# A two-layer mixer stack on one core: layer-0 scans with both directions in one tile, 64 x 64 matmuls, one mask per bank and the state's decay as a diagonal matmul

## The chip, the core and the metric

The kernel runs on one core of a Trainium2 chip, in one launch. The metric is the device time in microseconds. Three runs of the kernel before gave a median of 3486.47 us (3482.63 to 3488.52). The engines are named as in the profile: PE (matmuls), PEld (its weight loads), DVE (vector), ACT (scalar), POOL (GpSimd) and SP (which issues most transfers). PE's results go to PSUM, which the kernel divides into eight banks of 512 float32 columns.

## The reference, cut to what matters

A model with width 1024, 512 tokens (l) and 256 context tokens (c) runs through two layers of one kind and then two of another. The change is in the first layer's mixer, in its RWKV part: eight heads of 64 channels, each scanned over the context and then over the tokens, forwards and backwards.

```
def step(s, inp):                       # per head, s is [v, k]
    r_t, w_t, k_t, v_t, kk_t, b_t = inp
    sa = einsum('bhvk,bhk->bhv', s, kk_t)
    s = s * w_t - sa x b_t + v_t x k_t
    return s, einsum('bhvk,bhk->bhv', s, r_t)
for d in range(2):                      # direction 1 is reversed in time
    y_c, s_c = rwkv7_scan(*dir_inputs(prep_c, d), zeros)
    y_l, _   = rwkv7_scan(*dir_inputs(prep_l, d), s_c)
```

The same mixer has a spatial gate on the other half of the width, and both halves go through one output projection. The weights' GEMMs are split into two float32r parts, with three matmuls for a product.

## The kernel before, in words

**Chunks and blocks.** The scans work on chunks of 64 tokens. A strand of the program handles one pair of heads: head 0 lies on partitions 0 to 63, head 1 on 64 to 127. It goes through six blocks (two of the context, four of the tokens), and a block is two chunks (NB = 2) of each direction. So there are 4 x 6 = 24 blocks. A block has three parts.

`rwkv_prep` (L1009) loads keys, receptances and normalised keys (krk, one page per direction), makes two low-rank projections (`lora`, L1024; matmuls at L1030), the decays and their inverses, and the scaled operands b and kd (BK), direction by direction (L1069 to L1092). Then `products` (L1106) multiplies, per direction, chunk and head, 64 rows of [b, kd] (128 columns of weights) with 192 columns (decay matrix, r, kk): one matmul of the form 64 x 128 gives the token-major copies TM, the r products BI, and the kk products, from which the own half goes to W and the other half to KS. Each of these leaves PSUM through its own masked copy (L1116, twelve a block on DVE) or plain copy (L1122, four a block on ACT). L1137 multiplies kk with b again, in the other order, for L.

`Chunk.inverse` (L708) turns W into the transposed inverse of I + L by doubling, in five steps of two half steps. A half step is eight matmuls (four matrices, two heads) into one bank. Here the masked L and the intermediate product lie in padded pairs: head 0's page holds zeros on partitions 64 to 127 and the other way round, so that each matmul contracts 128 rows (form 128 x 64, L729 and L739). Masking on POOL (L721) and copying on ACT (L734) are one instruction per head. The second block kind of the kernel, from about 2300 us, calls the same function unpadded (form 64 x 64).

`rwkv_scan` (L1152) goes through two steps, in each one chunk of each direction: P = KS times [state over values], evicted by ACT to Pb; A = W times Pb, negated into NV by ACT and DVE; S = TM times NV, after which four DVE instructions (L1188, one per direction and head) decay the state with De and add S; and Y = BI times NV plus r times the old state, added to y.

**The order.** PE's order is fixed when the kernel is built. A strand is a generator: each `yield` states rough times (its own on PE, and the time until the next step finds its operands), and `tick` emits steps that are due between GEMM matmuls. Pairs 0 and 1 run under the projection and gate GEMMs; when these end (near 390 us), pairs 2 and 3 and a strand of modulation vectors (L539) start beside them. When pairs 0 and 1 have ended, `gemm_out` (L1269) starts its 288 GEMM matmuls beside the last blocks of pairs 2 and 3, and nothing of the mixer's output is normalised before pairs 2 and 3 have ended (`K.drain()`, near 920 us). Pairs 0 to 2 have two PSUM banks each; pair 3 has one, and a second when pair 0 ends.

Every product above is a float32 matmul, which the trace records as two passes. In the trace the passes of the two heads start within 0.01 us of each other and overlap.

## Time and profile before

| what | value |
|---|---|
| median of three runs | 3486.47 us |
| lowest, highest | 3482.63, 3488.52 us |
| profiled execution, its span | 3495.0 us |
| PE, DVE, ACT, POOL busy | 93%, 64%, 37%, 21% of the span |
| chain that ended last | PE 79%, DVE 12%, ACT 3%, DMA 2% |

The page gives no other time of the profiled execution than its span, which is 8.5 us above the median of the runs. The layer-0 scans lie in 120 to 925 us. A busy PE counts the time from a matmul's start to its modelled end, so that 90% is not 90% of its peak. The rows that matter are below.

### The profile page before, as it was taken

The page shows a single profiled execution, that of the slowest core. Times are in us where ns is not written, and L with a number is a line of the kernel's source. Part 1 is how long each engine was busy: PE and PEld are TensorE (multiplying, and loading weights), DVE is VectorE, ACT ScalarE, POOL GpSimd, SP SyncE. Part 2 cuts the span into 40 slices and gives each one's busy share as a digit, 9 for nine tenths or more (in the row PEclk, how much of TensorE's full clock was granted, in tenths as well). Part 3 has the DMA queues.
Part 4 walks back from the last instruction along what each step waited for, and adds up shares of the span by engine and source line. Part 5 has one row for each costly group of instructions (what it writes and reads, how often), then busy time and mean ns, then how long its engine had stood idle before and what let it go on. Part 6 is the DMA issues. An engine that isn't in the chain of part 4 may idle for free.

```text
span 3495.0 us, 60370 instructions
## 1 busy us (share of the span) xinstructions
PE 3253.1 (93%) x23708; PEld 2550.9 (73%) x23708; DVE 2231.2 (64%) x4937; ACT 1310.1 (37%) x2845; POOL 740.1 (21%) x982
## 2 busy tenths in 40 slices
PE   7999888979899999999988999988999998999998
PEld 5878666667678888877865788857767676766766
DVE  4544678774665555575666675767578566767655
ACT  4334344343342222246433332343333335234332
POOL 4222444432100000010000000004147100516600
PEclk8999989979899999999998999989999799999989
DMA  6432443531221212222222233232223153223333
GB/s 227 131 91 72 147 148 125 170 106 48 79 71 61 64 57 68 91 75 69 82 64 91 85 100 118 91 92 76 76 85 101 59 184 91 75 65 98 97 107 113
DMA packets 300511, 335.99 MB, mean 96 GB/s; under 512 B 25774, under 2 KB 246076, under 8 KB 300228
## 3 DMA queue, kind: packets, MB, share of 16 engines
q1 hardware_dynamic: 298116, 329.69, 29.6%
q8 instruction: 187, 3.06, 0.4%
q0 software_dynamic: 2112, 2.45, 0.3%
q14 instruction: 96, 0.79, 0.1%
HBM read 282.13 MB, written 49.94 MB: 95 GB/s over the span
## 4 chain that ended last, share of the span: by engine, by line
PE 79%; DVE 12%; ACT 3%; DMA 2%; issue 2%; POOL 1%; SPq 0%; DVEq 0%; POOLq 0%; ACTq 0%
PE mm L329 20%; PE mm L332 18%; PE mm L333 18%; PE ps L729 3%; PE ps L739 2%; PE ps L1164 2%; DVE cfa L1756 2%; PE ps L1110 2%; PE ps L539 1%; PE ps L371 1%; PE ps L2107 1%; DVE wl L78 1%; PE ps L1681 1%; PE ps L406 1%; PE ps L2094 1%
## 5 line engine op out<-in xcount | busy, mean ns | idle before, releaser
L329 PE MATMUL mm<-hl,wh 128*128 128x512 f32 (+1 forms) x3296 | 1254.4, 384 | 40.6 <-DVE qkv L1756 15.0
L332 PE MATMUL mm<-hl,wh 128*128 128x512 f32 (+1 forms) x3296 | 1224.6, 372 | 1.7 <-DVE hl L468 1.6
L333 PE MATMUL mm<-hl,wl 128*128 128x512 f32 (+1 forms) x3296 | 1216.6, 371 | 0.0
L329 PEld LDWEIGHTS mm<-hl,wh 128*128 128x128 f32 x3296 | 631.3, 192 | 181.8 <-issue 38.0
L333 PEld LDWEIGHTS mm<-hl,wl 128*128 128x128 f32 x3296 | 631.5, 192 | 113.5 <-issue 2.3
L332 PEld LDWEIGHTS mm<-hl,wh 128*128 128x128 f32 x3296 | 633.1, 192 | 101.5 <-DVE hl L468 3.2
L77 ACT ACTIVATE wh<-wr 128x512 fp32r<-128x512 f32 (+3 forms) x718 | 367.3, 561 | 680.8 <-PE mm L332 599.2
L78 DVE TENSOR_TENSOR wl<-wr,wh 128x512 fp32r<-128x512 f32 (+3 forms) x718 | 433.3, 637 | 220.8 <-ACT wh L77 199.7
L1334 DVE SCALAR_TENSOR_TENSOR cv<-mm,vecs,cv 128x441 f32<-128x441 f32 (+2 forms) x352 | 243.2, 692 | 94.1 <-ACT cv L1322 87.8
L1385 POOL MEMSET gwh<- 128x1024 f32 x3 | 2.9, 956 | 963.6 <-PE mm L332 963.6
L721 POOL TENSOR_TENSOR cut<-bk,zm 64x256 f32<-64x256 f32 x180 | 135.6, 753 | 145.4 <-PE ps L729 78.5
L1756 DVE SCALAR_TENSOR_TENSOR cfa<-ld,vecs,cfa 128x497 f32<-128x497 f32 (+14 forms) x160 | 151.2, 945 | 18.6 <-ACT cfa L1750 16.4
L1923 POOL TENSOR_SCALAR tap<-ld,vecs 128x498 f32<-128x498 f32 (+4 forms) x80 | 147.5, 1843 | 51.6 <-DVE kq L1982 12.4
L1357 DVE TENSOR_TENSOR fy<-fy,mm 128x512 f32<-128x512 f32 x96 | 55.2, 576 | 126.5 <-PE mm L333 125.7
L734 ACT ACTIVATE pad<-ps 64x256 f32<-64x256 f32 (+1 forms) x160 | 69.1, 432 | 152.0 <-PE ps L729 149.5
L1924 POOL TENSOR_TENSOR cfa<-cfa,tap 128x498 f32<-128x498 f32 (+4 forms) x80 | 115.8, 1447 | 5.5
L2099 ACT ACTIVATE u<-ps,beT 64x128 f32<-64x128 f32 x128 | 46.3, 362 | 153.1 <-DVE u L2098 152.0
L1110 PE MATMUL ps<-krk,bk 64*128 64x192 f32 x384 | 85.9, 410 | 13.9 <-ACT cut L1122 6.0
L351 POOL TENSOR_TENSOR rs<-var,mhalf 128x4 f32<-128x4 f32 (+1 forms) x26 | 28.8, 1107 | 313.9 <-DVE var L349 313.7
L729 PE MATMUL ps<-cut,cut 128*64 128x64 f32 x1440 | 92.4, 237 | 1.8 <-POOL cut L721 0.8
L1336 ACT ACTIVATE cv<-cv,vecs 128x256 f32<-128x256 f32 (+1 forms) x66 | 43.0, 652 | 133.2 <-DVE cv L1334 78.4
L729 PEld LDWEIGHTS ps<-cut,cut 128*64 128x64 f32 x1440 | 75.0, 147 | 13.6 <-issue 8.2
(479 smaller groups left out, 4761.3 us busy)
## 6 DMA issues: line engine op xcount, KB each, us to landing
ar<-in_ada_w_dram SPq DMA_DIRECT2D x96, 512.0 KB
wr<-in_ffn_up_dram SPq DMA_DIRECT2D x44, 1024.0 KB
wr<-in_w_in_dram SPq DMA_DIRECT2D x28, 1024.0 KB
ld<-sp SPq DMA_DIRECT2D x84, 256.0 KB
wr<-in_w_in_dram SPq DMA_DIRECT2D x32, 512.0 KB
xsp<-x SPq DMA_DIRECT2D x48, 256.0 KB
x<-xsp SPq DMA_DIRECT2D x48, 256.0 KB
wr<-in_ffn_down_dram SPq DMA_DIRECT2D x20, 512.0 KB
```

Source lines behind the costliest of these rows:

```text
L77: nc.scalar.activation(h[:, q:e], src, AF.Copy)
L78: nc.vector.tensor_tensor(l[:, q:e], src, h[:, q:e].bitcast(F32), SUB)
L329: mm = nc.tensor.matmul(ps[:m, :n], wh[:, i, :m], H[:, :n], start=first and i == 0, stop=False)
L332: nc.tensor.matmul(ps[:m, :n], wh[:, i, :m], L[:, :n], start=False, stop=False)
L333: nc.tensor.matmul(ps[:m, :n], wl[:, i, :m], H[:, :n], start=False, stop=last and i == nk - 1)
L721: nc.gpsimd.tensor_tensor(t[r].rearrange(T4, d=2, c=nb), Lp[r].rearrange(T4, d=2, c=nb), self.zm[s][r, ::-1].unsqueeze(2).to_broadcast([r. ...
L729: nc.tensor.matmul(ps[r, u * 64:u * 64 + 64], l[q, u], W[q, u], start=True, stop=True)
L1110: nc.tensor.matmul(ps[:, c], src, krk[d][hs[h]].rearrange("p x (c j) -> p x c j", c=NB)[:, :, c], start=True, stop=True)
L1334: nc.vector.scalar_tensor_tensor(t3[:, ro, co], a3[:, ri, ci], tap(ky, kx, ff), t3[:, ro, co], MUL, ADD)
L1756: nc.vector.scalar_tensor_tensor(dst[:, a:b], src[:, a + o:b + o], taps[j], dst[:, a:b], MUL, ADD)
L1923: nc.gpsimd.tensor_scalar(x[:, a:b], src[:, a + o:b + o], taps[j], None, MUL)
L1924: nc.gpsimd.tensor_tensor(g[:, a:b], g[:, a:b], x[:, a:b], ADD)
```

## The change

- b, kd, r, kk, decays and y of both directions lie in one tile each, so that what was done per direction is one instruction over 256 columns (`skew` gives access patterns that run over both directions' shifted decays; `both` and the y slice step from one direction's chunk to the other's). Two DVE instructions become ACT's (adding 1 to the decays' sigmoid, k_dir's scale and bias).
- `products` works with 64 x 64 matmuls: first, per head, b and kd times [r, kk] (128 columns) for all four chunks into one bank; one masked DVE instruction of 128 x 512 per bank (mask pm) then gives BI, the strict KS part and W's start. A second round (64 columns) with the diagonal decay matrices gives TM, after L1137's product. POOL's copies of kk into KS are two of 64 x 256 instead of four of 64 x 128. The low-rank matmuls are split into column halves.
- `inverse` is unpadded everywhere: 64 x 64 matmuls, one masking and one copy instruction for both heads.
- In the scan, the state's decay is a diagonal matmul into the bank of S (four more 64 x 64 matmuls a step), and two plain copies, one on ACT and one on DVE, take the new state out.
- The `yield` times of these steps are new. A strand of pairs 0 and 1 gets five half pages instead of six (the pool has 20, not 22), and the page with b and kd is freed before the scan, not after it. Comments and docstrings are removed, which shifts lines.

```diff
-        tri = K.const([P, 4, C64], name="tri")
...
+        pm = [K.const([P, 2, 2, C64], name="pm") for _ in range(2)]
+        nc.gpsimd.memset(pm[0], 1.0)
...
+            for d in range(2):
+                for x in range(2):
+                    sel(pm[0][r, d, x], [[1 - 2 * d, C64]], -x, 2 * d - 1)
+        nc.vector.tensor_copy(pm[1], pm[0])
...
+            nc.vector.tensor_copy(pm[h][r, :, 1], self.zm[1][r])
...
-            for r, _, t in own:
-                nc.gpsimd.tensor_tensor(t[r].rearrange(T4, d=2, c=nb), Lp[r].rearrange(T4, d=2, c=nb),
-                                        self.zm[s][r, ::-1].unsqueeze(2).to_broadcast([r.stop - r.start, 2, nb, C64]), MUL)
+            nc.gpsimd.tensor_tensor(Lm.rearrange(T4, d=2, c=nb), Lp.rearrange(T4, d=2, c=nb),
+                                    self.zm[s][:, ::-1].unsqueeze(2).to_broadcast([P, 2, nb, C64]), MUL)
...
-                for r, q, l in zip(hs, row, L):
-                    nc.tensor.matmul(ps[r, u * 64:u * 64 + 64], l[q, u], W[q, u], start=True, stop=True)
+                for r in hs:
+                    nc.tensor.matmul(ps[r, u * 64:u * 64 + 64], L[r, u], W[r, u], start=True, stop=True)
...
-            for r, z, _ in own:
-                nc.scalar.activation(z[r], ps[r], AF.Copy)
+            nc.scalar.activation(Zp, ps, AF.Copy)
...
+        for ds in (range(2),) if two else ((0,), (1,)):
+            ps = pss or {ds[0]: K.ps()[:, :n]}
+            for m in hs:
+                for d in ds:
+                    nc.tensor.matmul(ps[d][m], up[wkey][hs[d], m], at(lo[key], d)[hs[d]], start=True, stop=True)
+            for d in ds:
+                nc.scalar.activation(t[:, dsl(d)], ps[d], AF.Tanh, bias=K.v(bias, 4 * d + p), scale=0.5)
...
+    nc.vector.scalar_tensor_tensor(b, bI, 0.5, kk, MUL, MUL)
+    nc.vector.tensor_tensor(kI, kI, k, MUL)
+    nc.vector.tensor_tensor(kd, kI, iD, MUL)
...
+    for t, m in ((kk, skew(0, S + 1, C64)), (r, skew(1, S - 1, C64))):
+        t = t.rearrange(T4, d=2, c=NB)
+        nc.vector.tensor_tensor(t, t, m, MUL)
+    nc.vector.tensor_tensor(k.rearrange("p (u j) -> p u j", u=U), CH.i64.unsqueeze(1).to_broadcast([P, U, C64]),
+                            De.rearrange("p d c -> p (d c)").unsqueeze(2).to_broadcast([P, U, C64]), MUL)
...
-    def products(d, hh):
-        pss = [(h, K.ps()[:, :3 * n].rearrange("p (c x j) -> p c x j", c=NB, x=3)) for h in hh]
-        for c in range(NB):
-            for h, ps in pss:
-                src = BK[d][hs[h], c, h:h + 2].rearrange("p x j -> p (x j)")
-                nc.tensor.matmul(ps[:, c], src, krk[d][hs[h]].rearrange("p x (c j) -> p x c j", c=NB)[:, :, c],
...
-            masked(Wp[:, dsl(d)], own, 2, CH.zm[1][:, d])
-            masked(KS[h][d], opp, 2, CH.tri[:, 2 * d])
-            masked(BI[h][:, dsl(d)], slice(0, P), 1, CH.tri[:, 2 * d + 1])
-            nc.scalar.activation(TM[h][:, dsl(d)].rearrange(c4, c=NB), ps[:, :, 0], AF.Copy)
...
+    def products(hh, wd, rhs):
+        pss = {h: K.ps()[:, :U * wd] for h in hh}
+        for u in range(U):
+            for x in range(2):
+                for h in hh:
+                    src = (kd if x else b)[hs[h], 64 * u:64 * u + 64]
+                    nc.tensor.matmul(pss[h][hs[1 - h if x else h], wd * u:wd * u + wd], src, rhs(hs[h], u), start=True, stop=True)
+        return pss
...
+    for hh in ((0, 1),) if two else ((0,), (1,)):
+        pss = products(hh, 2 * C64, lambda q, u: KQ5[q, :, u])
+        for h in hh:
+            nc.vector.tensor_tensor(RK[h].rearrange("p (d c x) -> p d c x", d=2, c=NB),
+                                    pss[h].rearrange("p (d c x) -> p d c x", d=2, c=NB),
+                                    CH.pm[h].rearrange("p d x j -> p d (x j)").unsqueeze(2).to_broadcast([P, 2, NB, 2 * C64]),
+                                    MUL)
+        yield 500 * len(hh), 900
+    W = Wp[:, :2 * n].rearrange("p (u j) -> p u j", u=U)
+    KS = []
+    for h in range(2):
+        t = RK[h].rearrange(u4, u=U, x=2)[:, :, 1]
+        nc.vector.tensor_tensor(W[hs[h]], t[hs[h]], CH.i64[hs[h]].unsqueeze(1).to_broadcast([C64, U, C64]), ADD)
+        nc.gpsimd.tensor_copy(t[hs[h]], KQ5[hs[h], 1])
+        KS.append(t)
     ps = K.ps()
...
+    yield 320, 300
+    for hh in ((0, 1),) if two else ((0,), (1,)):
+        pss = products(hh, C64, lambda q, u: k[q, 64 * u:64 * u + 64])
+        for h in hh:
+            nc.scalar.activation(TM[h][:, :2 * n], pss[h], AF.Copy)
+        yield 320 * len(hh), 600
...
-        acc(pS, (lambda d, h: TM[h][:, u[d]], lambda d, h: NV[h][:, u[d]]))
-        for d in range(2):
-            for h in range(2):
-                q = hs[h]
-                nc.vector.scalar_tensor_tensor(SV[h][q, un[d]], SV[h][q, u[d]], De[q, d, cc[d]:cc[d] + 1], pS[q, d], MUL, ADD)
...
+        def decayed():
+            acc(pS, (lambda d, h: dg[hs[h], u[d]], lambda d, h: SV[h][hs[h], u[d]]), last=False)
+        if two:
+            decayed()
+        yield 320, 700
+        if not two:
+            decayed()
+        acc(pS, (lambda d, h: TM[h][:, u[d]], lambda d, h: NV[h][:, u[d]]), first=False)
+        nc.scalar.activation(slots(SV, 0, un), pS[hs[0]], AF.Copy)
+        nc.vector.tensor_copy(slots(SV, 1, un), pS[hs[1]])
...
+        t = y[s].rearrange("p (c j) -> p c j", j=C64)[:, o[0]:None if end < 0 else end:step]
+        if ("y", s, o[0]) in seen:
+            assert ("y", s, o[1]) in seen
...
```

PE's rows in the first scan step of the first pair (Pb: A's operand; the row after a row with the same tile is the same accumulation). Before (left out: the other strands' rows, and rows that repeat the pair above):

```order
L1164 MATMUL ps_2215<-Pb_2140,cut_1158 64x64 x4
...
L1164 MATMUL ps_2242<-cut_1156,cut_1160 64x64
L1164 MATMUL ps_2242<-cut_1157 64x64
...
L1164 MATMUL ps_2251<-cut_1159,cut_1156 64x64
L1164 MATMUL ps_2251<-cut_1160,cut_1157 64x64
...
L1164 MATMUL ps_2251<-krk_1296,cut_1155 64x64
L1164 MATMUL ps_2251<-krk_1296,cut_1156 64x64
```

The scan's own rows were A, S, then Y. Now, PE's rows at the same place (ps_2135 is S; its first four matmuls are the decay):

```order
L1176 MATMUL ps_2128<-Pb_2105,cut_1166 64x64 x4
L1176 MATMUL ps_2135<-cut_1161,cut_1163 64x64 x4
...
L1176 MATMUL ps_2135<-cut_1162,cut_1165 64x64
L729 MATMUL ps_2155<-pad_1641,bk_1684 64x64 x7
L1176 MATMUL ps_2135<-cut_1162,cut_1166 64x64
...
L1176 MATMUL ps_2165<-rk_1437,cut_1162 64x64
L1176 MATMUL ps_2165<-rk_1438,cut_1162 64x64
...
L1176 MATMUL ps_2165<-kq_1297,cut_1161 64x64 x4
```

The decay stands right behind A, in the same form (64 x 64), and S's product with TM (128 x 64) now meets a half step of the other strand's inverse in another form (L729, 64 x 64).

DVE's rows in the same step, before (cut_1157 is NV's second head, cut_1155 and cut_1156 the states, cut_1527 the other strand's W; the two L1188 rows come twice):

```order
L1181 TENSOR_SCALAR cut_1157<-ps_2215 64x2x64
L832 TENSOR_SCALAR kkv_2166<-ps_2161 128x8
L749 SCALAR_TENSOR_TENSOR k_2181<-mm_2029,vecs_109,k_2181 128x255
L1188 SCALAR_TENSOR_TENSOR cut_1155<-cut_1155,De_1321,ps_2242 64x64
L1188 SCALAR_TENSOR_TENSOR cut_1156<-cut_1156,De_1321,ps_2242 64x64
...
L740 TENSOR_TENSOR cut_1527<-cut_1527,ps_2265 128x256
```

The whole decay stood between NV and the other strand's row. DVE's rows of that step now (cut_1161 is the second head's state):

```order
L1195 TENSOR_SCALAR cut_1162<-ps_2128 64x2x64
L738 SCALAR_TENSOR_TENSOR k_2218<-mm_2082,vecs_109,k_2218 128x511
L730 TENSOR_TENSOR cut_1541<-cut_1541,ps_2155 128x256
L1208 COPY cut_1161<-ps_2135 64x128
L739 SCALAR_TENSOR_TENSOR k_2218<-mm_2082,vecs_109,k_2218 128x511
```

Four instructions have become one on DVE; the other half of the state is ACT's (L1207).

## Rows read from the trace of the kernel before

**Rows 1.** The page's part 4: shares of the chain that ended last, by engine

```profile
PE 79%; DVE 12%; ACT 3%; DMA 2%; issue 2%; POOL 1%; SPq 0%; DVEq 0%; POOLq 0%; ACTq 0%
```

**Rows 2.** Four stretches: length; busy PE, PEld, DVE, ACT, POOL; clock; DMA share; GB/s

```profile
180.00:390.00 210.00, 206.55 (x2075) 167.74 (x2076) 104.07 (x297) 80.16 (x196) 60.44 (x107) 1.00 0.30 90
390.00:680.00 290.00, 258.46 (x3774) 189.28 (x3773) 223.68 (x718) 118.99 (x390) 133.82 (x251) 0.88 0.44 145
680.00:780.00 100.00, 86.75 (x1347) 66.52 (x1343) 72.17 (x228) 42.73 (x132) 38.62 (x66) 0.86 0.43 129
780.00:925.00 145.00, 131.63 (x1376) 104.02 (x1377) 73.23 (x241) 47.57 (x133) 36.55 (x58) 0.90 0.15 47
```

**Rows 3.** Pieces of the chain of waits in 200 to 1000: start us, us, what

```profile
470.63 2.75 DMA krk<-rkv
...
776.75 2.65 DMA krk<-rkv
```

**Rows 4.** Timeline of PE from 694.46: start us, us, line, operation, shapes

```profile
694.46 0.44 PE L1137 MATMUL ps<-bk,krk 64*64 64x64 f32 x6
694.83 0.27 PE L729 MATMUL ps<-cut,pad 128*64 128x64 f32 x1
...
694.94 0.22 PE L729 MATMUL ps<-cut,pad 128*64 128x64 f32 x1
...
695.00 0.22 PE L729 MATMUL ps<-cut,pad 128*64 128x64 f32 x1
...
695.30 0.22 PE L729 MATMUL ps<-cut,cut 128*64 128x64 f32 x1
695.45 0.45 PE L1164 MATMUL ps<-Pb,cut 64*64 64x64 f32 x8
```

**Rows 5.** The same view: products of two heads at 833.79, of one at 432.07

```profile
432.07 0.92 PE L1110 MATMUL ps<-krk,bk 64*128 64x192 f32 x4
432.91 0.33 PE L739 MATMUL ps<-cut,bk 128*64 128x64 f32 x2
...
833.79 0.92 PE L1110 MATMUL ps<-krk,bk 64*128 64x192 f32 x8
834.64 0.50 PE L329 MATMUL mm<-hl,wh 128*128 128x512 f32 x1
```

**Rows 6.** The same view: 64 x 64 forms, both partition halves into one bank

```profile
260.73 0.68 PE L1137 MATMUL ps<-bk,krk 64*64 64x64 f32 x16
261.34 0.27 PE L1164 MATMUL ps<-cut,cut 128*64 128x64 f32 x1
...
2406.21 1.15 PE L729 MATMUL ps<-W,pad 64*64 64x64 f32 x32
```

**Rows 7.** DVE by line and shape, 160 to 960: xcount | busy us, mean ns | idle before

```profile
L1188 DVE SCALAR_TENSOR_TENSOR cut<-cut,De,ps 64x64 f32<-64x64 f32 x192 | 53.4, 278 | 21.6 <-PE ps L1164 18.9
L1116 DVE TENSOR_TENSOR cut<-ps,zm 64x128 f32<-64x128 f32 x92 | 26.3, 286 | 49.3 <-PE ps L1110 45.2 <-POOL cut L721 1.6 <-POOL bk L1103 1.0
L1089 DVE TENSOR_TENSOR krk<-krk,cut 128x128 f32<-128x128 f32 x92 | 25.3, 308 | 0.1
L1092 DVE TENSOR_TENSOR bk<-cut,cut 128x128 f32<-128x128 f32 x46 | 19.5, 424 | 0.0
L1073 DVE SCALAR_TENSOR_TENSOR cut<-cut,krk 128x128 f32<-128x128 f32 x46 | 14.3, 342 | 0.4 <-DMA krk<-rkv 0.3
L1133 DVE TENSOR_TENSOR cut<-cut,i 128x256 f32<-128x256 f32 x23 | 10.4, 451 | 0.0
...
L1246 DVE TENSOR_TENSOR gv<-ps,bs 128x512 f32<-128x512 f32 x4 | 2.7, 678 | 5.2 <-PE ps L1243 5.2
```

**Rows 8.** ACT by line and shape in the same stretch

```profile
L734 ACT ACTIVATE pad<-ps 64x256 f32<-64x256 f32 x120 | 45.3, 377 | 51.5 <-PE ps L729 49.1 <-PE ps L1164 0.5
L1180 ACT ACTIVATE cut<-ps 64x128 f32<-64x128 f32 x48 | 12.8, 268 | 24.8 <-PE ps L1164 24.3
L1141 ACT ACTIVATE bk<-ps 128x256 f32<-128x256 f32 x23 | 8.8, 383 | 15.9 <-PE ps L1137 15.1 <-PE ps L1110 0.7
```

More of the change, by code (lines that the diff above doesn't have):

```diff
@@ L737, in inverse @@
             for u in range(nu):
-                for r, q, z in zip(hs, row, Zv):
-                    nc.tensor.matmul(ps[r, u * 64:u * 64 + 64], X[q, u], z[q, u], start=True, stop=True)
+                for r in hs:
+                    nc.tensor.matmul(ps[r, u * 64:u * 64 + 64], X[r, u], Z[r, u], start=True, stop=True)
             nc.vector.tensor_tensor(Wp, Wp, ps, SUB)
@@ L875, in mixer_ab @@
         if p < 3:
-            strand(p - 1, p=6, h=6, halves=12)
+            strand(p - 1, p=6, h=5, halves=12)
         proj(p)
@@ new lines, in rwkv_prep, with both @@
+    loc_at = [o for _, o in loc]
+    def both(t, i):
+        o = [x // i for x in loc_at]
+        step = o[1] - o[0]
+        end = o[1] + (1 if step > 0 else -1)
+        return t.rearrange("p (c j) -> p c j", j=i)[:, o[0]:None if end < 0 else end:step]
+    bo = both(bon[s], n)
+    d2 = "p (d j) -> p d j"
+    if ("b", s, loc_at[0]) in seen:
+        assert ("b", s, loc_at[1]) in seen
+        rkp = K.p1(name="rk")
+        rk = rkp[:, :2 * n]
+        nc.vector.tensor_tensor(rk, r, kI, MUL)
+        nc.gpsimd.tensor_tensor(bo, bo, rk.rearrange(d2, d=2), ADD)
+        K.free(rkp)
+    else:
+        seen.update(("b", s, o) for o in loc_at)
+        nc.vector.tensor_tensor(bo, r.rearrange(d2, d=2), kI.rearrange(d2, d=2), MUL)
@@ new lines, in rwkv_prep @@
+    for t, m in ((kk, skew(0, S + 1, C64)), (r, skew(1, S - 1, C64))):
[3 more added lines that the diff above has]
+                            De.rearrange("p d c -> p (d c)").unsqueeze(2).to_broadcast([P, U, C64]), MUL)
+    K.free(csp, Dpp, bIp, kIp)
+    yield 250, 5000
+    RK = [K.p2(name="rk") for _ in range(2)]
+    TM = [K.p1(name="tm") for _ in range(2)]
@@ L1163, in acc @@
                 for h in range(2):
-                    nc.tensor.matmul(ps[hs[h], d], lhsT(d, h), rhs(d, h), start=i == 0 and d == 0,
-                                     stop=i == len(parts) - 1, skip_group_check=True)
+                    nc.tensor.matmul(ps[hs[h], d], lhsT(d, h), rhs(d, h), start=first and i == 0 and d == 0,
+                                     stop=last and i == len(parts) - 1, skip_group_check=True)
     for st in range(NB):
```

198 lines of the change are left out of this document (71 added, 127 removed).

## The prediction

> **What bounds the kernel now.** I read the chain that ended last first: PE holds 79% of it and DVE 12% [rows 1], so what counts is PE's time and the waits between PE's small groups of matmuls. The change touches only the layer-0 scans, so next I cut their time into stretches [rows 2]. In 180 to 390, where pairs 0 and 1 run under the projection GEMMs, PE is busy 206.55 of 210 us at full clock: only less PE work would help there. In 390 to 680 four strands and the modulation vectors run without GEMMs: PE is busy 258.46 of 290 us, DVE 223.68 of 290, and PE's granted clock is 0.88. In 680 to 780 two strands are left (PE 86.75 of 100, clock 0.86), and in 780 to 925 they share PE with `gemm_out` (131.63 of 145, clock 0.90). A clock of 0.88 means that the 1.2 GHz level had 24% of that stretch, the 2.4 GHz level the rest. So in the 535 us from 390 on PE stands idle for 31.5 + 13.3 + 13.4 = 58 us, and about 0.24 x 290 + 0.28 x 100 + 0.20 x 145 = 127 us pass at half clock. That is what a shorter chain can win, and PE is near enough to full that more work on it would cost.
>
> What sets the end of these 535 us is pairs 2 and 3: they start at 390, take six blocks one after the other, and `gemm_out`'s last matmuls and the norm wait for them. A block takes 535 / 6 = 89 us.
>
> **PE's own time.** Four edits change it.
>
> (1) Changes of form. PE's row-and-column form changes from 64 x 64 to 128 x 64 between 694.46 and 694.83 and back at 695.45 [rows 4]. Inside the 128 x 64 group a pair of passes starts every 0.06 us (694.94, 695.00). The first pass after the change is followed after 0.11 us (694.83 to 694.94), and the last is followed by the next form after 0.15 us (695.30 to 695.45). A change of form thus costs (0.11 - 0.06) + (0.15 - 0.06) = 0.14 us at full clock. I count the neighbours of different form in the two PE orders from the first product to the last matmul of `gemm_out`: 228 under the GEMMs, 407 between gate and `gemm_out` and 91 after, now 226, 293 and 85. That is 726 to 604, so 122 x 0.14 = 17 us less. The Trainium skill (TensorEngine Tiling (Array Packing), Key Properties) says that changing the tiling mode, not just the tile, drains the engine. It speaks against the change at one place, S with TM in 128 x 64 beside an inverse now in 64 x 64, and the trace agrees that a change is not free, at 0.14 us; but lora, products, inverse and A now share a form, and the count goes down.
>
> (2) The decay: 24 blocks x 2 steps x 4 matmuls x 2 passes = 384 passes, two side by side, so 192 x 0.06 = 11.5 us more. They stand behind A in A's form, so no change is added.
>
> (3) Products. A block has 8 matmuls of 192 columns in two passes. Two heads in turn, eight passes, take 834.64 - 833.79 = 0.85 us; one head alone takes 432.91 - 432.07 = 0.84 us for four passes [rows 5]. Side by side the second head is free. Without the change of form a pass takes (0.84 - 0.20) / 4 = 0.16 us. In the order 71 of the 192 matmuls stand beside the other head's, 37%, so a block is 0.37 x 1.28 + 0.63 x 2.56 = 2.1 us. Now there are 16 matmuls of 128 columns and 16 of 64. By 0.16 us for 192 and 0.06 for 64 columns, a pass of 128 is 0.11 us. No row shows two matmuls that share rows but write different column halves in the 64 x 64 form. If they run side by side, and the two heads too when they are in turn (222 of 384 and 137 of 384 in the order, 58% and 36%), a block is 0.58 x 0.88 + 0.42 x 1.76 + 0.36 x 0.48 + 0.64 x 0.96 = 2.0 us: no change. If they do not, everything doubles: 4.1 us, or 24 x 2.0 = 48 us more. The nearest rows are the padded passes of rows 4: two column halves, all rows in common, side by side. I take 0 and keep +48 as a bound. For the low-rank matmuls, twice as many with half the columns each, the same holds: 0, at worst 12 us more.
>
> (4) The unpadded doubling. Padded 128 x 64 pairs start every 0.06 us [rows 4]. In 64 x 64, 16 passes of L1137 take 261.34 - 260.73 = 0.61 us to the next form, so 7 steps of 0.06 and 0.2 around them; and the second block kind's unpadded half step of 32 passes takes 1.15 us with its tail [rows 6], again 0.06 a pair. So PE gains nothing from dropping the zeros. The Trainium skill (TensorEngine Tiling (Array Packing), Gotcha 1) says that different row tiles cannot access the same PSUM bank at the same time; unpadded, the two heads are two row tiles that write one bank. By that rule each of the 8 pairs would take 0.06 us more, in 240 half steps 115 us. The trace disagrees: rows 6 show just this form into one bank, at the pair's pace. It stays a rival with a small chance.
>
> PE in all: -17 + 11.5 + 0 + 0 = -6 us.
>
> **The chain between PE's groups.** Per block [rows 7, 8]:
> - State: four DVE instructions of 278 ns in a row, 1.11 us, become one on ACT (268 ns, the same shape as L1180) and one on DVE beside it: -0.84 us in each of two steps, -1.7.
> - Inverse: two ACT copies of 377 ns become one of 128 x 256 (L1141, 383 ns): -0.37 in each of five steps, -1.85. POOL's masks halve too; its work lies beside ACT's copy, the other product and DVE's subtraction, so I count nothing.
> - Masks: twelve L1116 of about 286 ns and W's 451 ns, 3.9 us, become two of 128 x 512 from PSUM (L1246, 678 ns) and two 64 x 256 priced as L1133: 2.3 us, -1.6.
> - Operands: four L1089, two L1092, two L1073, and two each of L1090 and L1070 priced as L1073: 1.23 + 0.85 + 3 x 0.68 = 4.1 us become six of 128 x 256, 2.7 us: -1.4.
>
> That is 6.5 us of 89 per block, and DVE loses about a third of its scan work. Pairs 2 and 3 pass six blocks: 39 us. I take 35, because the last block's steps lie under `gemm_out`, where PE is the limit. Under the projection GEMMs (180 to 390) I count nothing, since PE is full there; if it were not, 2 blocks x 6.5 would follow.
>
> Bounds: nothing at all if PE is the limit throughout, and 58 us idle plus half of 127 us at half clock, 121 us, if the chain no longer stops PE. The block's first loads of krk end the chain twice (2.75 and 2.65 us, [rows 3]) because their page was free only after Y; the page is now freed after the inverse. I count 0 and keep 6 x 2.7 = 16 us on the fast side. Waits that are added: TM's products need both banks back, so they wait for two masks in a row (1.4 us) and L's copy; queued behind them on PE are the other strands' steps. The copy of L, its mask on POOL and TM lie beside each other before the inverse, and I count 0; if TM's part, 0.36 x 0.48 + 0.64 x 0.96 = 0.8 us a block, were fully exposed on the late pairs, it would be 5 us.
>
> **Sum.** -6 - 35 = -41 us. The profiled execution spans 3495.0 us; that becomes 3454. It lies 8.5 us above the median of the runs, so the prediction is 3445 us.
>
> **Rivals.**
> - *DVE was the limit of the four-strand stretch.* For it: 77% busy with four strands queueing for it; then waits shrink by more than the durations, and PE, closer packed, keeps its 2.4 GHz level. Of the 121 us some 70 to 105 would be won, with the 6 us on PE: 3375 to 3410. Against it: DVE has only 12% of the chain [rows 1].
> - *Hidden anyway.* PE is 87 to 91% busy from 390 on, and its order is fixed beforehand; if what waits is its order and not its operands, only the -6 us and a few are left: 3475 to 3486.
> - *Slower: products that do not overlap.* Place: `products` and lora on PE. If two 64 x 64 matmuls that share a row half exclude each other, products cost +48 and lora +12 us; with -6 and half of the chain's gain (PE being fuller), -18, this is +36: 3522. It decides from a product pass pair of 0.11 us becoming 0.2: at 41 / 24 = 1.7 us more per block all is eaten. Against it are the padded pairs of rows 4.
> - *Slower: one bank, two row tiles* (the rule of the skill above): 3445 + 115 = 3560. Rows 6 stand against it.
>
> **How the numbers follow.** The forecast, 3410 to 3472 as its own range, 66%; DVE the limit 13%; hidden anyway 10%; products 9%; bank 1%; the last 1% for a slowdown that I did not see. A measurement of this kernel can tell 0.2% (7 us) from no change. Faster by over 0.2% (below 3479.5): 66 + 13 + 4 of the hidden case's 10 = 83, less 2 for the forecast's own spread, 81%. Within 0.2%: 8%. Slower: 11%. For 8 in 10 the range goes down into the DVE case, to 3397, and up over the hidden case, to 3488.
>
> **What would show it.** Right: the scans' end moves from 925 to near 884; L1208's copies (one a step) with the next KS product close behind; PE's busy time in the stage within 10 us of before; the new product line starting four passes within 0.03 us where heads are in turn; L720 and L729 pairs still 0.06 us apart; the granted clock in the stage not lower. Wrong: product passes at 0.2 us a pair (slower case); PE's idle time from 390 on still near 58 us with DVE far below 77% (hidden); the clock below 0.85, which would give back in PE time what the chain gains; or time that moves at any place after the scans, whose instructions are the same.

## The result, and the profile after

The changed kernel takes 3440.33 us (median of 4 runs, 3439.50 to 3442.73), the kernel before 3485.26 us: ratio 0.9866, 95% interval [0.9851, 0.9881]. The prediction was 3445 us. The profiled execution spans 3439.0 us, its mean granted clock is 0.952 (before 0.943).

Two rows per kernel cut the time into parts: the last matmul of the gate (end of the projection GEMMs) and the last matmul of the scans' ends. The fences hold one row for each, of before, then of after: line, engine, tile, count, duration in ns (least/median/most), first and last start in us.

```profile
L1243 PE MATMUL ps<-wsT,gvt x48: 270/276/378, 278.0 to 396.9; 128*128 128x128 f32 x48
...
L975 PE MATMUL ps<-ident,gn x288: 272/273/476, 346.6 to 918.9; 128*64 128x128 f32 x144
```

```profile
L1265 PE MATMUL ps<-wsT,gvt x48: 270/275/377, 272.4 to 398.9; 128*128 128x128 f32 x48
...
L965 PE MATMUL ps<-ident,gn x288: 272/273/476, 319.2 to 870.3; 128*64 128x128 f32 x144
```

The gate ends at 396.9 and 398.9. The stretch behind it, "the stage" from here on, takes 522.0 us before and 471.4 after. From the scans' end to the end of the span it is 2576.1 and 2568.7 us, of the same instructions. In the profiles of the runs below it is 2569.9 to 2580.5 us, but for one whose edit reaches there (experiment 4), so these 7.4 us are the scatter of single executions. So the gain is where it was looked for: 48.6 us at the scans' end by the two profiles, and 44.9 us in all by the medians. (The profiled execution of before was a long one: its span of 3495.0 us is above every run timed for this result.)

The chain after has nearly the shares of [rows 1], so it tells nothing of the gain:

```profile
PE 78%; DVE 11%; ACT 3%; DMA 3%; issue 2%; POOL 2%; SPq 0%; DVEq 0%; POOLq 0%; ACTq 0%
```

The stage as one window of each kernel, columns as in [rows 2], before and after:

```profile
397.00:919.00 522.00, 466.09 (x6440) 351.71 (x6439) 361.04 (x1160) 204.80 (x638) 206.91 (x371) 0.89 0.37 118
```

```profile
399.00:870.00 471.00, 417.55 (x7466) 325.80 (x7466) 262.91 (x678) 164.73 (x488) 117.08 (x203) 0.91 0.41 129
```

DVE lost 98 us, ACT 40, POOL 90. PE's records are busy for 48.5 us less, though there are a thousand more of them, and its idle time is 55.9 and 53.5 us, nearly the same. That reads as if PE had got less work, but this column cannot tell work from a short wait: a 64-column pass is recorded for 218 to 267 ns, but the next can start 30 to 60 ns after it, so a wait shorter than a record counts as busy. Counted from the starts of the stage's records, 1008 passes before start 0.13 to 0.5 us behind the one ahead of them, 232 us in all; after, 673, 141 us. Of these 91 us, 66 stand behind passes of the products and of the low-rank matmuls, whose old form was 64 x 128; the distances below 0.13 us grew from 198 to 231 us. How much of what went was waiting and how much was the passes' own time, the starts do not say. (The Trainium skill, Perfetto Trace Analysis, Identifying the Most-Contended Engine, calls the busy share of matmuls no good measure of how close a kernel is to its roofline, because they are pipelined; this case agrees: 48.5 us of "busy" time went while the records became more.)

The DVE and ACT rows that answer to [rows 7, 8], 160 to 960:

```profile
L1128 DVE TENSOR_TENSOR rk<-ps,pm 128x512 f32<-128x512 f32 x46 | 30.5, 686 | 20.9 <-PE ps L1121 19.2 <-PE ps L1024 0.8 <-PE ps L720 0.8
L1137 DVE TENSOR_TENSOR cut<-rk,i 64x256 f32<-64x256 f32 x46 | 22.5, 490 | 1.2
L1102 DVE TENSOR_TENSOR kq<-kq,cut 128x256 f32<-128x256 f32 x46 | 21.2, 486 | 0.1
L1208 DVE COPY cut<-ps 64x128 f32<-64x128 f32 x48 | 14.1, 295 | 24.0 <-ACT cut L1207 23.1
...
L1076 DVE TENSOR_TENSOR bk<-cut,cut 128x256 f32<-128x256 f32 x23 | 9.6, 416 | 0.0
...
L724 ACT ACTIVATE cut<-ps 128x256 f32<-128x256 f32 x60 | 22.7, 382 | 51.9 <-PE ps L720 47.2 <-PE ps L729 2.6 <-PE ps L1121 1.9
L1207 ACT ACTIVATE cut<-ps 64x128 f32<-64x128 f32 x48 | 13.0, 270 | 32.6 <-PE ps L1176 32.2
```

The mean durations are those of the prediction within 0.05 us (masks 686 for 678, copies 382 for 383). The order is not: L1208 waits for ACT's L1207. The prediction had the two halves of the state beside each other. The trace of before had shown that DVE's copy of A's second half waits for ACT's copy of the first (L1180), in the view of [rows 7]:

```profile
L1181 DVE TENSOR_SCALAR cut<-ps 64x128 f32<-64x128 f32 x48 | 14.0, 294 | 23.9 <-ACT cut L1180 22.7
```

The timeline after shows the state's halves one behind the other too, as it shows A's (now L1194, L1195); columns start us, us, engine, line:

```profile
500.60 0.27 ACT L1194 ACTIVATE cut<-ps 64x128 f32<-64x128 f32 x1
...
500.91 0.29 DVE L1195 TENSOR_SCALAR cut<-ps 64x128 f32<-64x128 f32 x1 [3.21 <-ACT cut L1194]
...
505.08 0.27 ACT L1207 ACTIVATE cut<-ps 64x128 f32<-64x128 f32 x1
...
505.38 0.29 DVE L1208 COPY cut<-ps 64x128 f32<-64x128 f32 x1 [0.65 <-ACT cut L1207]
```

The new products do run four abreast. In the second round of one block, where both heads are in turn, 32 passes of 64 columns take 0.52 us to the next line (838.85 to 839.37), against 0.85 us for eight passes of 192 columns of two heads before [rows 5]; four single records start within 0.03 us, the next four 0.11 us after the first four, and from there on four more every 0.06 us. (PE's timeline after; the first two rows are the doubling, for a point further down.)

```profile
503.99 0.68 PE L720 MATMUL ps<-cut,cut 64*64 64x64 f32 x16
504.60 0.39 PE L1176 MATMUL ps<-cut,cut 128*64 128x64 f32 x5
...
838.85 0.70 PE L1121 MATMUL ps<-cut,bk 64*64 64x64 f32 x32 [0.31 <-DVE rk L1128]
839.37 0.41 PE L1176 MATMUL ps<-Pb,cut 64*64 64x64 f32 x8
```

### The profile page after: what moved, and what is told of

It reads as the page before. It is cut to its first block, busy times and chain, and to the rows that moved or that the text cites. A ratio compares the mean times of both kernels' runs of the same rounds, so it can differ in the third digit from the quotient of the medians.

```text
span 3439.0 us, 62780 instructions
## 1 busy us (share of the span) xinstructions
PE 3202.1 (93%) x25436; PEld 2523.3 (73%) x25436; DVE 2121.8 (62%) x4341; ACT 1272.1 (37%) x2679; POOL 628.5 (18%) x762
## 4 chain that ended last, share of the span: by engine, by line
PE 78%; DVE 11%; ACT 3%; DMA 3%; issue 2%; POOL 2%; SPq 0%; DVEq 0%; POOLq 0%; ACTq 0%
PE mm L329 20%; PE mm L332 18%; PE mm L333 18%; PE ps L720 2%; PE ps L1176 2%; PE ps L729 2%; DVE cfa L1778 2%; PE ps L1121 1%; PE ps L539 1%; PE ps L371 1%; PE ps L2128 1%; DVE wl L78 1%; PE ps L1703 1%; PE ps L2115 1%; PE ps L2142 1%
## 5 line engine op out<-in xcount | busy, mean ns | idle before, releaser
L724 ACT ACTIVATE pad<-ps 128x256 f32<-128x256 f32 (+1 forms) x100 | 46.7, 467 | 150.9 <-PE ps L720 147.9
L406 PE MATMUL ps<-sq,one 128*128 128x512 f32 (+1 forms) x132 | 64.0, 625 | 18.9 <-ACT sq L376 17.2
L730 DVE TENSOR_TENSOR cut<-cut,ps 128x256 f32<-128x256 f32 x120 | 49.3, 415 | 51.4 <-PE ps L729 49.9
L1362 DVE TENSOR_TENSOR cv<-cv,mm 128x512 f32<-128x512 f32 x66 | 39.5, 599 | 65.5 <-ACT cv L1358 35.4
L2119 DVE TENSOR_SCALAR u<-ps,kdT 64x128 f32<-64x128 f32 x128 | 44.7, 349 | 52.1 <-PE ps L2115 41.8
```

## The experiments

Each kernel was timed against the kernel before on its own chip. Two ratios can be compared to about 0.25% (9 us), so each run is also read at the scans' end of its profile, where the rest of the kernel adds no noise. One profile each is no interval either: in the stage the clock alone differs between runs (0.86 to 0.94). The profiled execution lies within 5 us of its run's median, except in experiment 6 (10.6 us below) and in the third run of experiment 7 (8.5 us below).

**1. Only the numbers behind yield.** The edits of the change also carry new planned times. They do no work; they set where the strands' pieces stand between the GEMMs in PE's fixed order. The changed kernel with the old numbers, and the kernel before with the new ones:

```diff
-    yield 250, 5000
+    yield 430, 5000
...
-        yield 500 * len(hh), 900
+        yield 320 * len(hh), 1500
...
-    yield 320, 300
+    yield 320, 1500
```

> The changed kernel with the numbers behind yield as they were before the change (they only set where the strands' pieces stand in PE's order). In the order 4 blocks of the scans then stand ahead of the last gate matmul, as in the kernel before; with the new numbers 5 do. The forecast's theory (shorter chain of pairs 2 and 3, nothing from the projection GEMMs): no change, 3440 us within 7, ratio 0.985 to 0.989. Rival, the lead: the fifth block under the GEMMs costs nothing there and is missing later, where 20 blocks took 522 us, 26 us a block: 3440 + 20 to 26 = 3460 to 3466 us, ratio 0.992 to 0.995.

> The kernel before with the new numbers behind yield and nothing else. In the order 5 blocks stand ahead of the last gate matmul instead of 4. The forecast's theory: the instructions are the same, so no change, 3485 us, ratio 0.998 to 1.002. The lead: 26 us less at most, 3459 to 3470 us, ratio 0.992 to 0.996; if the GEMM phase grows by the block's PE time, 12 us, half of that is lost.

Measured: 0.9891 [0.9867, 0.9915] with the changed kernel's instructions, 0.9968 [0.9955, 0.9982] with those of before. Their two rows, old numbers first:

```profile
L1265 PE MATMUL ps<-wsT,gvt x48: 270/275/377, 270.7 to 390.7; 128*128 128x128 f32 x48
...
L965 PE MATMUL ps<-ident,gn x288: 272/273/477, 338.1 to 879.8; 128*64 128x128 f32 x144
```

```profile
L1243 PE MATMUL ps<-wsT,gvt x48: 271/275/378, 272.5 to 408.4; 128*128 128x128 f32 x48
...
L975 PE MATMUL ps<-ident,gn x288: 272/273/477, 327.8 to 907.6; 128*64 128x128 f32 x144
```

With the two kernels of the result this is a table of two by two (us):

| | gate's end | stage | scans' end |
|---|---|---|---|
| before | 396.9 | 522.0 | 918.9 |
| before, new numbers | 408.4 | 499.2 | 907.6 |
| changed, old numbers | 390.7 | 489.1 | 879.8 |
| changed | 398.9 | 471.4 | 870.3 |

At the scans' end the numbers alone bring 11.3 and 9.5 us, the instructions alone 39.1 and 37.3; by the ratios it is 11 and 9, 38 and 36. The two hardly depend on each other. Of the instructions' gain 6.2 and 9.5 us are there already at the gate's end, with the same blocks ahead of it; 32.9 and 27.8 us lie in the stage. With the new numbers five blocks instead of four stand ahead of the gate's last matmul. That lengthens the GEMM phase by 11.5 and 8.2 us and shortens the stage by 22.8 and 17.7. Both theories were half wrong: the forecast's 0 and the lead's 20 to 26.

**2. More of the same.** The factor on the early strands' planned waits, `SL1`, from 0.9 to 0.6: seven blocks ahead of the gate's last matmul.

> The changed kernel with the factor on the two early strands' planned waits under the projection GEMMs at 0.6 instead of 0.9. In the order 7 blocks stand ahead of the last gate matmul instead of 5. The forecast's theory (PE is full under the GEMMs): the GEMM phase grows by what the stage after it loses, no change, ratio 0.985 to 0.989. The lead: two more blocks hidden; 25 us less for each if they cost the GEMM phase nothing (3390 us, ratio 0.973), 13 us for each if they cost it their 12 us of PE streaming (3415 us, ratio 0.980). Slower, over 3450 us, if the planned waits are now shorter than the real ones and PE's order stalls the GEMMs.

Measured 0.9945 [0.9927, 0.9963]: 28 us slower than the changed kernel. The gate ends at 447.3 (48.4 us later), the stage takes 453.9 (17.5 less). The two further blocks cost the GEMM phase 24 us each and give back 9, with a clock in the stage of 0.86 for 0.91. PE's row for that phase shows no sign of it:

```profile
180.00:447.00 267.00, 260.56 (x3388) 210.55 (x3384) 122.01 (x291) 106.11 (x255) 53.31 (x97) 0.98 0.27 81
```

PE is "busy" 98% here, as it was before (206.55 of 210, [rows 2]), where a further block fitted in for 8 to 12 us. Full by this column says nothing of how much fits. Why the next two blocks cost twice as much, no run here shows.

**3. A dose on DVE, off the chain.** After each transpose in the scans' doubling, a second one into a tile that nothing reads.

```diff
             nc.vector.transpose(Xp, Wp)
+            if n == 256:
+                nc.vector.transpose(self.spare, Wp)
```

> The changed kernel with a second transpose of W (into a spare tile that nothing reads) behind each transpose of the scans' doubling: five of 0.45 us a block on DVE, 2.25 us, beside the ACT copy and the second product, so not on the block's own chain. Forecast's theory (the chain): at most 5 us, 3440 to 3445, ratio 0.986 to 0.989. Rival, DVE is the limit of the four-strand stretch: some 13 blocks pass there, 13 x 2.25 = 29 us, and up to 19 x 2.25 = 43 us over the whole stage: 3469 to 3483 us, ratio 0.995 to 0.999.

Measured 0.9906 [0.9885, 0.9928], 14 us slower; scans' end 880.7, 10.4 later, of which 1.6 us are there at the gate's end (400.5). The added instructions (120 to 960):

```profile
L726 DVE STREAM_TRANSPOSE spare<-cut 128x256 f32<-128x256 f32 x120 | 49.6, 413 | 0.9
```

The dose was smaller than planned. Each starts 0.37 us behind the transpose ahead of it, whose record is 0.44 us long, so the records overlap, and DVE is busy 291 us in the stage for 263: 1.5 us more for each of its 19 blocks, not 2.25. Too much for work that is hidden, far too little for DVE as the limit. Six blocks of 1.5 us are 9 us, which is what the stage lost: DVE work beside the block's own chain costs about as much as work on it. That this is so because it stands in one queue with the other strands' work is a reading; no run tested it by itself.

**4. The doubling's copy in two halves again.**

```diff
-            nc.scalar.activation(Zp, ps, AF.Copy)
+            for r in hs:
+                nc.scalar.activation(Zp[r], ps[r], AF.Copy)
```

> The changed kernel with the doubling's ACT copy again in two halves of 64 x 256, one after the other, and nothing else: about 0.37 us more between the two products of each half step, five a block. Forecast's theory (late pairs' chain): 5 x 0.37 x 6 blocks = 11 us more, ratio 0.990 against 0.9866 of the changed kernel. Rival, hidden (PE has other strands' work in that time): 0 to 3 us, ratio 0.9866 to 0.9875. DVE is not touched, so the DVE theory also says 0.

Measured 0.9945 [0.9929, 0.9961], 27 us slower. The function also serves layer 1, where the kernel before had one copy already; from the scans' end on this kernel takes 18 us more than the changed one (2586.6 to 2568.7). The scans' end, 882.1, is 11.8 us later, at the same clock (0.92 to 0.91). That is the chain's 11 us, and hidden is refuted; but 5.4 of the 11.8 us are there at the gate's end (404.3), where the forecast counted nothing, and the stage took only 6.5 us longer.

**5. The state's decay back on DVE.**

```diff
-        acc(pS, (lambda d, h: TM[h][:, u[d]], lambda d, h: NV[h][:, u[d]]), first=False)
-        nc.scalar.activation(slots(SV, 0, un), pS[hs[0]], AF.Copy)
-        nc.vector.tensor_copy(slots(SV, 1, un), pS[hs[1]])
+        acc(pS, (lambda d, h: TM[h][:, u[d]], lambda d, h: NV[h][:, u[d]]))
+        for d in range(2):
+            for h in range(2):
+                q = hs[h]
+                nc.vector.scalar_tensor_tensor(SV[h][q, un[d]], SV[h][q, u[d]], De[q, d, cc[d]:cc[d] + 1], pS[q, d], MUL, ADD)
```

> The changed kernel with the state's decay back in four DVE instructions a step and without the diagonal matmuls. Forecast's theory: the chain loses 2 x 0.84 us a block again, 6 x 1.7 = 10 us, and PE gets its 11.5 us of decay matmuls back, of which part counts: between -2 and +5 us, ratio 0.986 to 0.988. With the two halves one after the other, as the trace after shows them (0.27 + 0.03 + 0.29 us), the chain term is 2 x 0.52 x 6 = 6 us: -5 to +1 us, ratio 0.985 to 0.987. Rival, DVE's load counts wherever it lies, at the rate of the dose run (about 14 us for 24 x 2.25 us): 24 x 2 x 0.82 = 39 us of load, +10 us, ratio 0.989 to 0.990.

Measured 0.9887 [0.9869, 0.9906], scans' end 872.9: 7 us by the one, 2.6 by the other, at a clock of 0.89 for 0.91. The decay on PE gains little; none of the three expectations is excluded.

**6. Masks and operands in pieces.** Eight masks of 128 x 128 for two of 128 x 512, the four operand products per direction.

```diff
+            for d in range(2):
+                for x in range(2):
+                    a, m = [t.rearrange("p (d c x j) -> p d c x j", d=2, c=NB, x=2)[:, d, :, x] for t in (RK[h], pss[h])]
+                    nc.vector.tensor_tensor(a, m, CH.pm[h][:, d, x].unsqueeze(1).to_broadcast([P, NB, C64]), MUL)
```

> The changed kernel with the masks in eight DVE instructions of 128 x 128 instead of two of 128 x 512, and the four operand products per direction, eight of 128 x 128 instead of four of 128 x 256. By the rows of the two traces 8 x 0.31 - 2 x 0.69 = 1.1 us and 8 x 0.32 - 4 x 0.48 = 0.65 us more on DVE and on the block's chain, 1.75 us a block. Forecast's theory: 6 x 1.75 = 10.5 us, ratio 0.9896. DVE's load at the dose run's rate: 24 x 1.75 x 0.3 = 13 us, ratio 0.990 (the two can't be told apart here). Rival, hidden: 0 to 3 us, ratio 0.9866 to 0.9875.

Measured 0.9862 [0.9844, 0.9880], within 2 us of the changed kernel: not slower. The scans' end, 859.0, is that of the shortest of five executions, at a clock of 0.94, and says little. The expectation had the wrong prices: it added up the durations of single instructions. The masks' pieces in the stage of this run:

```profile
L1132 DVE TENSOR_TENSOR rk<-ps,pm 128x128 f32<-128x128 f32 x144 | 30.7, 281 | 14.8 <-PE ps L1122 14.7
```

144 records of 281 ns cover 30.7 us, 0.21 us each, because those that follow one another overlap. DVE's busy time in the stage rose by 8 us (262.9 to 271.2), 0.4 us a block, not 1.75. So this run undoes little, and what the wide masks and operands are worth by themselves stays open.

**7. PE's forms.** First the two products of y in turn by direction, 87 more changes of form; then the low-rank matmuls in their old form, 93 more; then their new form in the kernel before, none more.

```diff
-        acc(pY, (lambda d, h: NV[h][:, u[d]], lambda d, h: BI[h][:, u[d]]),
-            (lambda d, h: SV[h][hs[h], u[d]], lambda d, h: r[hs[h], u[d]]))
+        for d in range(2):
+            for h in range(2):
+                nc.tensor.matmul(pY[hs[h], d], NV[h][:, u[d]], BI[h][:, u[d]], start=d == 0, stop=False, skip_group_check=True)
+            for h in range(2):
+                nc.tensor.matmul(pY[hs[h], d], SV[h][hs[h], u[d]], r[hs[h], u[d]], start=False, stop=True, skip_group_check=True)
```

> The changed kernel with the two products of y in turn by direction (128 x 64, 64 x 64, 128 x 64, 64 x 64 instead of each form once): the same matmuls, 87 more changes of form in PE's order (691 to 604). At 0.14 us each 12 us of PE time, where PE's time counts: the forecast's PE term says +9 to +12 us, ratio 0.989 to 0.990. Rival, a change of form hides in PE's waits: 0 to 4 us, ratio 0.9866 to 0.988.

```diff
-            for m in hs:
-                for d in ds:
-                    nc.tensor.matmul(ps[d][m], up[wkey][hs[d], m], at(lo[key], d)[hs[d]], start=True, stop=True)
+            for d in ds:
+                nc.tensor.matmul(ps[d], up[wkey][hs[d]], at(lo[key], d)[hs[d]], start=True, stop=True)
```

> The changed kernel with the low-rank matmuls as before the change: one of 64 x 128 for each direction instead of two of 64 x 64, nothing else. PE's order then has 93 more changes of form (697 to 604). The forecast counted nothing for these matmuls and 0.14 us for a change of form: +13 us, ratio 0.990. New theory, PE's own passes: in the trace of before two passes of one such matmul start 0.213 us apart and nothing runs beside them, 8 pairs in a block's two calls, in the trace after four 64 x 64 passes share that time; with the forms the line's share of PE in the stage was 31.4 us before and 14.7 after: +17 us in the stage and some +3 under the GEMMs, +20 us, ratio 0.992 to 0.993, and the scans' end at 888 to 892 us instead of 870. Rival, only the chain between PE's groups counts: 0 to 3 us.

> The kernel before with the low-rank matmuls as the change has them, two of 64 x 64 for each direction, and nothing else. Its order has as many changes of form as before (731 to 726), since the products, the doubling and most of the scan stay in other forms. The forecast's terms (0 for the matmuls, 0.14 us a change): no change, ratio 0.999 to 1.002. New theory, PE's passes by themselves: 8 passes of 0.213 us a block become 32 of about 0.03, 1.7 to 0.9 us, 0.8 us a block, 20 blocks in the stage: 16 us less, and 3 under the GEMMs, ratio 0.994 to 0.996. If both hold and the gain of the low-rank matmuls was all in the changes of form, ratio 0.999 to 1.001 here and 0.990 to 0.993 in the other run.

Measured 0.9910 [0.9891, 0.9928] and 15.9 us at the scans' end for the first: 0.17 to 0.18 us a change, in the scan. The starts of y's passes show the price by themselves: from the first to the last of a step's 16 it is 0.61 us in the changed kernel (median of 48 steps) and 0.91 us here, for two more changes, 0.15 us each. 0.9883 [0.9862, 0.9903] and 4.9 us for the second: 0.05 to 0.06 us a change, in the low-rank matmuls, not clear of the changed kernel by the ratio, and all at the gate's end (403.7); the stage takes 471.5 us, as in the changed kernel. 1.0024 [1.0012, 1.0037] for the third, 8 us slower than before, which no theory had; its scans' end, 3.1 us earlier, is that of the shortest of twelve executions. No gain. The new theory, that the low-rank line's share of PE (31.4 us of the stage before, 14.7 after, counted to the next start) is time gained, falls: it promised 20 and 16 us. In the second run the share rose to 22.6 us and the stage stayed as long, so other lines' shares took it over.

**8. A's halves in two banks.**

```diff
-        pA = new()
-        acc(pA, (lambda d, h: W[hs[h], u[d]], lambda d, h: Pb[hs[h], d]))
-        nc.scalar.activation(slots(NV, 0, u), pA[hs[0]], AF.Copy, scale=-1.0)
-        nc.vector.tensor_scalar(slots(NV, 1, u), pA[hs[1]], -1.0, None, MUL)
+        pA = [new(), new()] if two else [new()] * 2
...
+        nc.scalar.activation(slots(NV, 0, u), pA[0][hs[0]], AF.Copy, scale=-1.0)
+        nc.vector.tensor_scalar(slots(NV, 1, u), pA[1][hs[1]], -1.0, None, MUL)
```

> The changed kernel with the two heads' halves of A in two PSUM banks (strands that have two), so that ACT's copy of one half and DVE's of the other read different banks. In the trace after, DVE's copy starts 0.03 us after ACT's ends (500.60 + 0.27, then 500.91), in every step. If the shared bank's tile is what makes it wait, DVE's copy now starts with ACT's, the chain is 0.3 us shorter in each of two steps a block: 6 x 0.6 = 3.6 us less for the late pairs, ratio 0.985 to 0.987. If the wait has another cause, the copies stay one behind the other and the time does not change. Slower, 0.988 or more, if the second bank is not free in time and A's matmuls wait for it.

Measured 0.9849 [0.9825, 0.9872], scans' end 864.6. DVE's two copies by line and shape in the stage of this run:

```profile
L1197 DVE TENSOR_SCALAR cut<-ps 64x128 f32<-64x128 f32 x38 | 11.2, 295 | 21.4 <-PE ps L1195 16.5 <-ACT cut L1196 4.1
L1210 DVE COPY cut<-ps 64x128 f32<-64x128 f32 x38 | 11.2, 295 | 19.2 <-ACT cut L1209 18.7
```

A's half (L1197) now waits mostly for PE; the state's (L1210), still in one bank, waits for ACT as before. So the shared tile of a bank makes the second reader wait. The 5.7 us at the scans' end are within what one profile can scatter of the 3.6 expected; against the changed kernel the ratio alone is not clear.

**9. Two DVE instructions a block to POOL as well.**

```diff
-    for t, m in ((kk, skew(0, S + 1, C64)), (r, skew(1, S - 1, C64))):
+    for e, t, m in ((nc.gpsimd, r, skew(1, S - 1, C64)), (nc.vector, kk, skew(0, S + 1, C64))):
...
-        nc.vector.tensor_tensor(W[hs[h]], t[hs[h]],
+        (nc.vector, nc.gpsimd)[h].tensor_tensor(W[hs[h]], t[hs[h]],
```

> The run with A's halves in two banks, and of each block two DVE instructions on POOL instead: r times its decays (0.50 us on DVE) and W's addition for the second head (0.49 us). POOL is busy 117 of the stage's 471 us in the trace after; there an addition of 128 x 256 takes it 0.87 us. The theory that every microsecond taken from a block's DVE or ACT work is worth the six blocks of a late pair (the dose run: 2.25 us a block gave 10 us at the scans' end; the two copies: 1.85 us gave 12): about 1.0 us x 6 = 6 us below the two-bank run, ratio 0.982 to 0.984, and DVE's busy time in the stage 18 us lower. Rival, DVE's work is hidden and only PE's time counts: no change, 0.985. Rival, POOL becomes late (r's product waits 0.87 us for it instead of 0.5): 2 to 4 us slower, 0.986.

Measured 3428.80 us, 0.9827 [0.9809, 0.9846], scans' end 854.1: 10.5 us below the two-bank run, 16.2 below the changed kernel. This version beats the changed kernel: its interval lies wholly below that one's. Against the two-bank run the ratio alone is not clear. The stage's window (401 to 854) and four rows:

```profile
401.00:854.00 453.00, 406.64 (x7449) 317.24 (x7449) 248.05 (x641) 162.69 (x487) 140.72 (x239) 0.94 0.43 134
```

```profile
L1102 POOL TENSOR_TENSOR kq<-kq,cut 128x256 f32<-128x256 f32 x18 | 14.5, 805 | 7.7 <-DVE bon L1098 6.2 <-DVE cut L1098 1.5
L1137 POOL TENSOR_TENSOR cut<-rk,i 64x256 f32<-64x256 f32 x18 | 13.5, 750 | 36.6 <-DVE rk L1128 34.1 <-ACT Pb L1190 2.1
...
L1102 DVE TENSOR_TENSOR kq<-kq,cut 128x256 f32<-128x256 f32 x18 | 12.6, 698 | 0.1
L1137 DVE TENSOR_TENSOR cut<-rk,i 64x256 f32<-64x256 f32 x18 | 9.1, 505 | 0.2
```

DVE's busy time fell by 13.6 us (261.6 in the two-bank run's stage), not by 18, because the halves that stayed take longer: L1102 698 ns and L1137 505, for 569 and 422 in the two-bank run's stage.

## Why the prediction was right

**The chain between PE's groups** came out in size, but not where the forecast had it. The run with the old numbers has as many blocks in its stage as before; there DVE is busy 266.3 us and ACT 168.8, 94.7 and 36.0 less than before, 131 us over 20 blocks, 6.5 us a block. The scans end 39.1 us earlier, six times that, at a clock of 0.90 for 0.89. But 6.2 of the 39.1 us are there at the gate's end, and the stage is 32.9 us shorter, five times 6.5; with the new numbers it is 9.5 and 27.8. The forecast had 35 + 6 in the stage and nothing ahead of it. Two runs put such time back: 1.85 us a block on ACT cost 11.8 us at the scans' end, 6.5 of them in the stage; 1.5 on DVE cost 10.4, some 9 in the stage. So an edit counted six to seven blocks' worth at the scans' end, and 3.5 to 6 in the stage. Why that many, when DVE is busy only 62% from 399 to 680 (172.95 of 281)? The late pairs take their blocks one after the other, and each waits for the engines in turn; that is a reading, not shown. The dose shows that "on the chain" was too narrow: it counts beside it, too, on DVE.

**Luck.** That 3445 lies within 5 us of the result is in part chance. By the ratios the instructions bring 36 to 38 us, for the 41 forecast. The numbers behind yield, which the forecast left out, bring 9 to 11 more.

**Its parts** were less right than their sum. The copies: 11 us predicted for the late pairs, 11.8 shown at the scans' end, 6.5 in the stage. The state: mis-sized, since its two halves run one behind the other: 0.27 + 0.03 + 0.29 us for 1.11, 0.52 us a step saved and not 0.84, so 1.0 us a block, not 1.7; the run without it lost 3 to 7 us, PE's 11.5 us of decay matmuls taken off. Masks and operands, 18 us predicted: not shown; the run meant for them put back too little. The operands were mis-sized, because their price was a sum of durations, and short records that follow one another overlap (in [rows 7] 92 of L1089's 308 ns cover 25.3 us, not 28.3): by what the records cover they took 3.5 us a block and take 2.9 now, 0.6 saved and not 1.4. That 6.5 us a block came out all the same is owed to edits that were not priced, such as the additions into y and the copies of TM, where one instruction now does the work of two.

**PE's -6 us** is not shown either. The 0.14 us a change of form agrees with the starts of y's passes (0.15), but as time of the kernel the runs show 0.18 at one place and 0.05 at another; why the place matters so much stays open. Low-rank matmuls at 0 stand: their form in the kernel before brought nothing. Products that exclude each other are refuted by the starts of the passes: four 64 x 64 passes start within 0.03 us. Products at 0 are not shown: with as many blocks in the stage (new numbers, before and changed) their line's share of PE, counted to the next start, fell from 62.0 to 49.2 us, and no run put the old products back, so whether that is time gained or passes to other lines, as the low-rank share did, stays open. The other slower rival, one bank for two row tiles, falls with the doubling after, whose two heads write one bank: 16 passes take 0.61 us to the next line (503.99 to 504.60), the time of 16 passes in [rows 6].

**The step that failed** is "Under the projection GEMMs (180 to 390) I count nothing, since PE is full there". PE's busy column was taken to mean that nothing can be won there. In its place the runs show two gains. The changed instructions brought the gate's end forward by 6.2 and 9.5 us, with the same blocks ahead of it and at a clock of 0.99 to 1.00 in each. And the new numbers behind yield, which the prediction left out, moved one block more ahead of it, at 8.2 and 11.5 us there for 17.7 and 22.8 in the stage, which gave 9.5 to 11.3 us. Whether PE had room or only did the same work sooner is open; what was wrong was to count nothing. The fallback of 13 us that the prediction named for "if it were not" has the right cause and is too large.

**Two of the signs it named** misled. PE's busy time in the stage was to stay within 10 us and fell by 48.5; PE's idle time at 58 us with DVE far below 77% was to mean "hidden anyway", and stands at 53.5 with DVE at 62% while the time fell as forecast. Both take a record's length for PE's time. A clock "not lower" held: 0.91 for 0.89, that is 18% of 471 us at the 1.2 GHz level for 22% of 522, 30 us less, worth up to 15 us of PE time by that estimate. Whether the denser passes earned that or chance did, no run here separates; in the runs the stage's clock went from 0.86 to 0.94. It is not the main cause, since with the old numbers the instructions' 39.1 us came at 0.90 for 0.89.

The rival "DVE was the limit" does not fit the size of the dose: 10 to 14 us, for the 20 to 29 us that 1.5 us in each of its 13 to 19 blocks would be.

## What to carry to other kernels

Where strands share in-order queues, price an edit by what it takes off the engines' work in a block, times the blocks that the last strand passes, whether the instruction lies on that strand's own path or beside it; here that gave the time at the scans' end, though part of it was won ahead of the stretch where it was looked for. Take the price of short instructions from what their records cover, not from a sum of durations. Don't read room from a matmul engine's busy share; look at the starts of its passes, or put one more piece of work there and time it. When a change also edits the numbers that a planner orders by, run the numbers alone: here they were a fifth of the gain, and a factor of the same kind that moved two more blocks lost 28 us.

## What the runs showed of the hardware

- Two engines that read two partition halves of one PSUM tile ran one behind the other, 0.03 us apart where nothing else held the second one (L1194 and L1195, L1207 and L1208); in two banks DVE's copy of A's half waited 4.1 us in all for ACT, for 33.8 in the changed kernel (160 to 960). The rows name ACT's instruction as what released DVE, by its semaphore; whether the memory would need that no run here tried without it. The Trainium skill (PSUM — Partial Sum Buffer, PSUM bank collisions raise a hardware error) says that engines may access one bank at the same time in different quadrants.
- DVE's multiplication of 128 x 256 (L1102) took 410 ns with POOL idle (mean of 31 of 48 in the changed kernel). In the last run it took 877 to 947 ns in 10 of the 11 cases in which a POOL multiplication or addition of 128 x 256 had begun less than 0.2 us ahead of it. The Trainium skill (GPSIMD Engine Reference, Specifications) names the shared access for DVE instructions with two SBUF inputs; the trace agrees. The scans still ended 10.5 us earlier.
- Short DVE instructions that follow one another overlap in their records: pieces of 128 x 128, recorded for 281 ns each, covered 0.21 us each.
- A change of PE's row-and-column form between passes of y cost 0.15 us by the passes' starts.
- Four 64 x 64 f32 matmuls, two row halves by two column halves, ran abreast (32 passes of 64 columns in 0.52 us), and two row halves writing one bank started 7 ns apart (L720, 840.127 and 840.134).
